# Earlier first loads, the norm as a row, and gate work laid between projection pieces in a hybrid encoder block

## The chip, the cores and the metric

The kernel runs on one NeuronCore of one Trainium2 chip. The metric is device time in microseconds (us) of one launch; lower is better. The times before are the median of three runs; one further execution was taken with the hardware profiler, and everything said of single instructions comes from it.

Five engines work side by side, each on its own queue in order: TensorE (PE in the profile, its weight loads PEld) multiplies and transposes, VectorE (DVE) and ScalarE (ACT) do elementwise work, GpSimd (POOL) fills and issues some transfers, SyncE (SP) issues most DMA transfers. PE writes to PSUM, eight banks of 128 x 512 fp32.

## The reference

All of it is fp32, with 256 tokens and a model width of 2048. The layer is a modulated block with two parallel sequence mixers:

```python
mod = silu(c) @ ada_w + ada_b                     # shift, scale, gate for two sub-layers
h = rms_norm(x, norm_mix_w) * (1 + scale_m) + shift_m
proj = h @ w_in                                   # one wide projection
...
h_a = bidirectional(mlstm_chunkwise, (q_a, k_a, v_a), ...)       # 4 heads, input and forget gates
qkv = silu(centred_depthwise_conv(b_qkv, gdn_conv_w))            # 5 taps along the tokens
beta = sigmoid(dir_heads(b_beta, B_HEADS))
log_decay = -exp(A_log) * softplus(dir_heads(b_a, B_HEADS) + dt_bias)
o_b = bidirectional(gated_delta_chunkwise, (q_b, k_b, v_b), ...)  # 16 heads
y_b = (rms_norm(o_b) * silu(b_z)) @ w_branch_b
...
x = x + gate_m * ((g_a * y_a + g_b * y_b) @ w_out)
x = x + gate_f * SwiGLU(rms_norm(x) * (1 + scale_f) + shift_f)
out = rms_norm(x, norm_final_w)
```

`proj` is split into q, k, v, output gate and gates of the mLSTM branch, q|k|v, z, beta and decay of the delta-rule branch ("heads" below), and merge gates.

## The kernel before

**Front (lines 73 to 98).** The vector c is loaded as one row `c1` of a 32-row zeroed tile, on ACT's DMA queue behind nothing in the program (the scheduler put it third, behind `cst` and `pk`). PE multiplies it by ones to spread it over 128 partitions; a Silu writes `row_c`. `c1` has a pool of its own, `w00`, which is closed at line 98, so that its space goes to the next pool, `w0`.

**First projection (lines 236 to 276).** Both halves of x, token by token in rows, are loaded as `xt` (1 MB each, SP queue). ACT squares them with a running sum (into parts of `x` as a throw-away), takes the root; DVE inverts it and scales `xt` by it; PE transposes `xt` in 32 pieces, ACT copies the results to `x` (channels on partitions, 16 blocks of 128 channels x 256 tokens). Then, for each block b of 16: two rows of `ada2` (`ra`, 1 MB each) and 16 column blocks of `w_in` (`raw`, 1 MB) are loaded; DVE forms the block's scale and shift as products with `row_c` (line 270), ACT applies both at once (line 271), `split` writes the block as a high part `hh` (ACT) and a rest `hl` (DVE), and PE accumulates 16 outputs `first[o]` in all eight banks with plain fp32 matmuls (line 274). `ra` has five slots (the two `xt` use the first two), `raw` has three.

**Gates (lines 279 to 344).** `first[0]` holds the gate pre-activations, `first[1..12]` q, k, v of heads 0 to 3, `first[13..15]` a part of the mLSTM's q and k. `gdn_conv` (line 217) evicts one output twice (to a padded tile and, scaled by the centre tap, to `cv`), adds four taps on DVE, and applies a Silu. Six convolutions come first in the program, then the gates: a polynomial for softplus, exponentials, `alpha_d` to DRAM (from where `gdn_phase1` reads it back), two scans, and the transpose `ptr` that yields `bT`, `eT` and `mT`.

**The rest of the projection in pieces.** `fjob` and `tjob` (lines 122 and 143) are generators. A `tjob` takes four 1 MB loads `raw`, and for each half load makes a high part `wh` (ACT, line 153) and a rest `wl` (DVE, line 154), three slots each, then issues 12 matmuls (lines 159 to 161): one piece. z of the delta-rule branch, v, the output and merge gates are such jobs. `fills` is the list of jobs with no deadline, and `fill(n)` takes n pieces. After the gates the program runs the eight pieces of z's first job, takes two fill pieces, and then (lines 637 to 644) works through heads 0 to 3 (`gdn_phase1`) and the first block inversion with fill pieces between their steps.

**What sets the order.** The Tile framework places instructions on each engine's queue by program order as a priority, but lets one that its own timing model sees ready go ahead of one that is not; waits are put in by it. A tile of a rotating pool waits until the last user of its slot is done. A DMA that waits for a slot holds up all later ones of its queue.

Of the kernel before, what the change touches and what calls it, by code (L numbers as in the profile page):

```python
# [9 lines left out]
F32 = mybir.dt.float32  # L10
# [40 lines left out]
def hybrid_block(ctx: ExitStack, tc: tile.TileContext, xr, nfr, crow, pk_d, cst_d, ada2, ada4, win0, winb, wint, wba, wbb, wo, wgu, wd, out, dbg=None):  # L51
# [16 lines left out]

    def gps(name):
        return g_ps.tile([P, 512], F32, tag="g", name=name)  # L70
# [23 lines left out]
    for g in range(4):  # L94
        pc_ = acc_ps.tile([P, 512], F32, tag="acc", name=f"crow{g}")
        PE.matmul(pc_, ones[0:32], c1[:, g * 512 : (g + 1) * 512], start=True, stop=True)
        S.activation(row_c[:, g * 512 : (g + 1) * 512], pc_, AF.Silu)
    s0.close()
# [44 lines left out]
    def tjob(name, chunks, xh, xl, done):  # L143
# [3 lines left out]
        for u, src in enumerate(chunks):  # L147
            raw = st.tile([P, 4, 512], F32, tag="raw", bufs=3, name=f"raw_{name}_{u}")
            nc.sync.dma_start(raw, src)
            for k0 in range(0, 4, 2):  # L150
                wh = st.tile([P, 2, 512], F32R, tag="wh", bufs=3, name=f"wh_{name}_{u}_{k0}")
                wl = st.tile([P, 2, 512], F32R, tag="wl", bufs=3, name=f"wl_{name}_{u}_{k0}")
                S.activation(wh, raw[:, k0 : k0 + 2], AF.Copy)  # L153
                V.tensor_tensor(wl, raw[:, k0 : k0 + 2], wh.bitcast(F32), ALU.subtract)  # L154
                for k in range(2):
                    kk = 4 * u + k0 + k
                    for t in range(2):
                        c = slice(t * P, (t + 1) * P)
                        PE.matmul(ps[t], xh[:, kk, c], wh[:, k], start=kk == 0, stop=False)  # L159
                        PE.matmul(ps[t], xl[:, kk, c], wh[:, k], start=False, stop=False)  # L160
                        PE.matmul(ps[t], xh[:, kk, c], wl[:, k], start=False, stop=kk == last)  # L161
                if k0:
                    pump()
                    if u == len(chunks) - 1:
                        done(ps)
                yield True
# [43 lines left out]
    NP_ = 3  # L210
# [6 lines left out]
    def gdn_conv(h, j, ps):  # L217
# [13 lines left out]
        S.activation(cv, ps, AF.Copy, scale=w[2])  # L231
# [3 lines left out]

    with ExitStack() as s0:
        w0 = pool(s0, "w0")

        x = w0.tile([P, KB, T], F32, name="x")
        ss = w0.tile([P, 2], F32, name="ssx")  # L240
        xt = []
        for t in range(2):
            xt.append(w0.tile([P, D + 2], F32, tag="ra", bufs=5, name=f"xt{t}"))
            nc.sync.dma_start(xt[t][:, :D], xr[:, t])
        for t in range(2):
            junk = x[:, 8 * t : 8 * t + 8].rearrange("p b t -> p (b t)")
            S.activation(junk, xt[t][:, :D], AF.Square, accum_out=ss[:, t : t + 1])
        S.activation(ss, ss, AF.Sqrt, bias=epsc, scale=1.0 / D)
        V.reciprocal(ss, ss)
        for t in range(2):  # L250
            V.tensor_scalar(xt[t][:, :D], xt[t][:, :D], ss[:, t : t + 1], None, ALU.mult)
        for b2 in range(KB // 2):
            px = gps(f"pxx{b2}")
            for e in range(2):
                for t in range(2):
                    PE.transpose(px[:, e * T + t * P : e * T + (t + 1) * P], xt[t][:, (2 * b2 + e) * P : (2 * b2 + e + 1) * P], ident)
            S.activation(x[:, 2 * b2 : 2 * b2 + 2], px.rearrange("p (e t) -> p e t", e=2), AF.Copy)
        banks = [acc_ps.tile([P, 512], F32, tag="acc", name=f"first{i}") for i in range(4)]
        banks += [gps(f"first{i}") for i in range(4, 8)]
        first = [banks[o // 2][:, (o % 2) * T : (o % 2 + 1) * T] for o in range(N0)]  # L260
        for b in range(KB):
            ra = [w0.tile([P, D + 2], F32, tag="ra", bufs=5, name=f"ra{b}_{i}") for i in range(2)]
            for i in range(2):
                nc.sync.dma_start(ra[i], ada2[b, :, i])
            raw = st.tile([P, N0, P], F32, tag="raw", bufs=3, name=f"raw0_{b}")
            nc.sync.dma_start(raw, win0[b])
            m2 = w0.tile([P, 2], F32, tag="m2", bufs=3, name=f"m2_{b}")
            for i in range(2):
                f = 1.0 if i else pk[:, PK_NMIX + b : PK_NMIX + b + 1]
                V.scalar_tensor_tensor(ra[i], ra[i], f, row_c, ALU.mult, ALU.mult, accum_out=m2[:, i : i + 1])  # L270
# [761 lines left out]
```

## Time and profile before

| | |
|---|---|
| median of three runs | 2219.57 us (2217.16 to 2230.97) |
| the profiled execution | 2226.21 us, span of its instructions 2224.4 us |
| PE busy | 2096.3 us, 94% of the span |
| DVE, ACT, POOL busy | 1408.9, 994.9, 103.6 us |
| read from HBM | 467.21 MB, 218 GB/s over the span |
| mean granted TensorE clock | 0.979 |
| PE's wait for `c1`, then for the transposes | 10.4 us, 14.0 us |
| PE's wait for the first split of z | 7.4 us |

The profile gives, for each group of instructions, its line, engine and operation, the tiles out<-in, shapes, count, busy us and mean ns, and after a second bar the idle time of the engine before them with what ended it. The timeline gives start and duration in us from the first instruction. In the stretches, the busy time of each engine is given with a count, then the granted clock (1.00 is full), the share of the DMA engines' time, and GB/s.

### The profile page before, as it was taken

What the parts mean: (1) busy time and instruction counts of PE and PEld (TensorE: products, weight loads), DVE (VectorE), ACT (ScalarE), POOL (GpSimd) and SP (SyncE); (2) the same over time, 40 slices, a digit from 0 to 9 for tenths busy, and PEclk for the clock granted to TensorE, in tenths of its full rate; (3) what the DMA queues carried; (4) which work ended last, traced back from release to release, by engine and by line L of the source; (5) the groups of instructions that cost most, each with busy time, mean ns of one, the idle gap of its engine ahead of it and who ended that gap; (6) DMA issues with size and microseconds to landing.
All of it is one profiled execution on the core that took longest, in us unless ns stands there. A gap on an engine that the chain in (4) does not pass through costs nothing.

```text
span 2224.4 us, 27756 instructions
## 1 busy us (share of the span) xinstructions
PE 2096.3 (94%) x10756; PEld 1754.7 (79%) x10756; DVE 1408.9 (63%) x2120; ACT 994.9 (45%) x1399; POOL 103.6 (5%) x206
## 2 busy tenths in 40 slices
PE   5989989998998899989999999989999999999997
PEld 4867778978887888778787787868888888878886
DVE  4677777886788677845557776564544454454454
ACT  3146436644564456434443444444444444444443
POOL 0002101100210111010000000000000000000000
PEclk9999999999999999999999999999999999999999
DMA  8976665675667455756787676545555555555553
GB/s 308 416 303 194 184 215 187 204 248 191 192 236 241 163 189 205 255 201 231 286 318 269 241 291 232 186 141 191 190 183 191 191 190 183 192 199 189 192 197 122
DMA packets 82645, 485.83 MB, mean 218 GB/s; under 512 B 10681, under 2 KB 21057, under 8 KB 28113
## 3 DMA queue, kind: packets, MB, share of 16 engines
q1 hardware_dynamic: 68672, 459.34, 58.0%
q0 software_dynamic: 6496, 9.49, 2.7%
q10 hardware_dynamic: 7346, 15.24, 1.8%
q8 instruction: 84, 1.38, 0.2%
q14 instruction: 47, 0.39, 0.0%
HBM read 467.21 MB, written 16.82 MB: 218 GB/s over the span
## 4 chain that ended last, share of the span: by engine, by line
PE 60%; DVE 4%; DMA 3%; issue 2%; ACT 1%; POOL 0%; DVEq 0%; ACTq 0%; POOLq 0%
PE acc_gt L159 4%; PE acc_gt L160 4%; PE acc_up L161 4%; PE acc_up L160 4%; PE acc_up L159 4%; PE acc_d L160 4%; PE acc_gt L161 4%; PE acc_d L159 4%; PE acc_d L161 4%; PE acc_o L160 2%; PE acc_o L161 2%; PE acc_o L159 2%; DMA ada<-ada 1%; PE acc_ya L160 1%; PE acc_ya L159 1%
## 5 line engine op out<-in xcount | busy, mean ns | idle before, releaser
L154 DVE TENSOR_TENSOR wl_up<-raw_up,wh_up 128x1024 fp32r<-128x1024 f32 x88 | 107.9, 1226 | 128.7 <-ACT wh_up L153 128.7
L154 DVE TENSOR_TENSOR wl_d<-raw_d,wh_d 128x1024 fp32r<-128x1024 f32 x88 | 107.8, 1226 | 123.2 <-ACT wh_d L153 123.2
L154 DVE TENSOR_TENSOR wl_gt<-raw_gt,wh_gt 128x1024 fp32r<-128x1024 f32 x88 | 107.8, 1225 | 109.3 <-ACT wh_gt L153 109.3
L107 DVE SCALAR_TENSOR_TENSOR ada<-ada,crow 128x2048 f32<-128x2048 f32 x64 | 146.2, 2284 | 39.2 <-DMA ada<-ada 39.2
L135 PE MATMUL acc_b<-hh,wh_b 128*128 128x256 f32 x576 | 167.3, 290 | 0.0
L137 PE MATMUL acc_b<-hh,wl_b 128*128 128x256 f32 x576 | 162.5, 282 | 1.1 <-DVE wl_b L132 1.1
L136 PE MATMUL acc_b<-hl,wh_b 128*128 128x256 f32 x576 | 162.9, 283 | 0.0
L153 ACT ACTIVATE wh_d<-raw_d 128x1024 fp32r<-128x1024 f32 x88 | 93.3, 1061 | 138.9 <-PE acc_d L160 132.0
L153 ACT ACTIVATE wh_gt<-raw_gt 128x1024 fp32r<-128x1024 f32 x88 | 93.3, 1060 | 133.9 <-PE acc_gt L160 78.9
L153 ACT ACTIVATE wh_up<-raw_up 128x1024 fp32r<-128x1024 f32 x88 | 93.2, 1060 | 117.8 <-PE acc_up L160 84.6
L159 PE MATMUL acc_gt<-wh_gt,hfh 128*128 128x512 f32 x352 | 138.8, 397 | 1.3 <-ACT hfh L183 1.1
L160 PE MATMUL acc_gt<-wh_gt,hfl 128*128 128x512 f32 x352 | 139.4, 396 | 0.0
L161 PE MATMUL acc_gt<-wl_gt,hfh 128*128 128x512 f32 x352 | 138.7, 394 | 0.0
L159 PE MATMUL acc_d<-wh_d,ffh 128*128 128x512 f32 x352 | 137.4, 390 | 0.0
L160 PE MATMUL acc_d<-wh_d,ffl 128*128 128x512 f32 x352 | 137.4, 390 | 0.0
L161 PE MATMUL acc_d<-wl_d,ffh 128*128 128x512 f32 x352 | 137.0, 389 | 0.0
L161 PE MATMUL acc_up<-wl_up,hfh 128*128 128x512 f32 x352 | 136.9, 389 | 0.0
L159 PE MATMUL acc_up<-wh_up,hfh 128*128 128x512 f32 x352 | 136.9, 389 | 0.0
L160 PE MATMUL acc_up<-wh_up,hfl 128*128 128x512 f32 x352 | 136.9, 389 | 0.0
L274 PE MATMUL first<-x,raw 128*128 128x256 f32 x512 | 111.6, 380 | 2.0 <-ACT x L271 2.0
L135 PEld LDWEIGHTS acc_b<-hh,wh_b 128*128 128x128 f32 x576 | 110.6, 192 | 2.1 <-issue 1.4
L137 PEld LDWEIGHTS acc_b<-hh,wl_b 128*128 128x128 f32 x576 | 110.8, 192 | 1.7 <-DVE wl_b L132 1.7
(339 smaller groups left out, 5375.8 us busy)
## 6 DMA issues: line engine op xcount, KB each, us to landing
ada<-ada SPq DMA_DIRECT2D x64, 1024.0 KB, 5.4
raw_gt<-wgu SPq DMA_DIRECT2D x44, 1024.0 KB, 4.9
raw_up<-wgu SPq DMA_DIRECT2D x44, 1024.0 KB, 4.9
raw_d<-wd SPq DMA_DIRECT2D x44, 1024.0 KB, 4.8
raw_b<-winb SPq DMA_DIRECT2D x36, 1024.0 KB, 5.4
ra<-ada SPq DMA_DIRECT2D x32, 1025.0 KB, 12.7
raw<-win SPq DMA_DIRECT2D x16, 1024.0 KB, 10.5
raw_z<-wint SPq DMA_DIRECT2D x16, 1024.0 KB, 5.8
```

Source lines behind the costliest of these rows:

```text
L107: V.scalar_tensor_tensor(raw, raw, 1.0, row_c[:, :D], ALU.mult, ALU.mult, accum_out=mod[:, c0 + b : c0 + b + 1])
L135: PE.matmul(o, wh[:, k], hh[:, kk], start=kk == 0, stop=False)
L136: PE.matmul(o, wh[:, k], hl[:, kk], start=False, stop=False)
L137: PE.matmul(o, wl[:, k], hh[:, kk], start=False, stop=kk == KB - 1)
L153: S.activation(wh, raw[:, k0 : k0 + 2], AF.Copy)
L154: V.tensor_tensor(wl, raw[:, k0 : k0 + 2], wh.bitcast(F32), ALU.subtract)
L159: PE.matmul(ps[t], xh[:, kk, c], wh[:, k], start=kk == 0, stop=False)
L160: PE.matmul(ps[t], xl[:, kk, c], wh[:, k], start=False, stop=False)
L161: PE.matmul(ps[t], xh[:, kk, c], wl[:, k], start=False, stop=kk == last)
L274: PE.matmul(first[o], raw[:, o], x[:, b], start=b == 0 and o % 2 == 0, stop=b == KB - 1 and o % 2 == 1)
```

## The change

`c1` becomes one row in a slot of `raw`, first on ACT's queue and without zeroed rows; the matmul contracts over one row. SP's order is pinned: both `xt`, then for each block `raw` before its two `ra`. `xt` is transposed as loaded, and DVE, not ACT, evicts the transposes; the inverse root becomes a row over the tokens, spread over the partitions by a matmul with a diagonal (`dg`, `rows`), and enters each block in one new DVE operation together with the scale; ACT then adds only the shift. The rest `hl` of a block is taken one block later. The squares go to a third slot of `ra` (`junk`).

`tjob` gets `early`: so many first splits are made, pinned in order, before its banks are taken; z's first job makes three. z and the fill jobs are in `fills` before the gates start. The gates become a generator with twelve steps, one piece after each, the six convolutions standing between the gate operations. `evict` copies the outputs to four pads (three before) ahead of the convolutions, which read the centre tap from the pad. Where before eight pieces of z and two more ran before the heads, now eight and four do. The job definitions move up unchanged.

`order(ins)` pins an instruction behind the one that precedes it in the program on its engine; it adds no wait.

```diff
-    s0 = ExitStack()
-    w00 = pool(s0, "w00")
-    c1 = w00.tile([32, D], F32, name="c1")
-    V.memset(c1, 0.0)
-    S.dma_start(c1[0:1], crow.unsqueeze(0))
+    c1 = st.tile([1, D], F32, tag="raw", bufs=3, name="c1")
+    S.dma_start(c1, crow.unsqueeze(0))
...
-        PE.matmul(pc_, ones[0:32], c1[:, g * 512 : (g + 1) * 512], start=True, stop=True)
+        PE.matmul(pc_, ones[0:1], c1[:, g * 512 : (g + 1) * 512], start=True, stop=True)
...
+        def halves(u, k0):
...
+            order(S.activation(wh, raws[u][:, k0 : k0 + 2], AF.Copy), early)
+            order(V.tensor_tensor(wl, raws[u][:, k0 : k0 + 2], wh.bitcast(F32), ALU.subtract), early)
+            return wh, wl
+
+        todo = [(u, k0) for u in range(len(chunks)) for k0 in (0, 2)]
+        made = [halves(*q) for q in todo[:early]]
+        if early:
+            yield True
...
-    NP_ = 3
+    NP_ = 4
...
+        if ps is not None:
+            S.activation(pd[:, 2 : T + 2], ps, AF.Copy)
         cv = fr.tile([P, T], F32, tag="cv", bufs=2, name=f"cv{h}_{j}")
-        S.activation(pd[:, 2 : T + 2], ps, AF.Copy)
-        S.activation(cv, ps, AF.Copy, scale=w[2])
+        S.activation(cv, pd[:, 2 : T + 2], AF.Copy, scale=w[2])
...
+        if ps is None:
+            evict(3 * h + j + 1 + NP_)
...
+    def gates(w0, zz, first):
+        evict(1)
+        order(V.tensor_scalar(zz, first[0], pk[:, PK_GB : PK_GB + 1], sgn, ALU.add, ALU.mult))
+        for o in range(2, NP_ + 1):
+            evict(o)
...
+        S.activation(tr[0:32, 0], zz[0:32], AF.Sigmoid)
+        yield
+        gdn_conv(0, 0, None)
+        yield
...
+            order(nc.sync.dma_start(xt[t][:, :D], xr[:, t]))
+        junk = w0.tile([P, D + 2], F32, tag="ra", bufs=5, name="junk")
+        for t in range(2):
+            order(S.activation(junk[:, :D], xt[t][:, :D], AF.Square, accum_out=ss[:, t : t + 1]))
...
+            V.tensor_copy(x[:, 2 * b2 : 2 * b2 + 2], px.rearrange("p (e t) -> p e t", e=2))
+        V.reciprocal(ss, ss)
+        dg = w0.tile([P, T], F32, name="dgx")
+        for t in range(2):
+            V.tensor_scalar(dg[:, t * P : (t + 1) * P], ident, ss[:, t : t + 1], None, ALU.mult)
+        prow = acc_ps.tile([P, 512], F32, tag="acc", name="prow")
+        PE.matmul(prow[:, :T], ones, dg, start=True, stop=True)
+        order(S.activation(rows, prow[:, :T], AF.Copy))
...
+            order(nc.sync.dma_start(raw, win0[b]))
+            for i in range(2):
+                order(nc.sync.dma_start(ra[i], ada2[b, :, i]))
+            m2 = w0.tile([P, 2], F32, tag="m2", bufs=3, name=f"m2_{b}")
+            f = pk[:, PK_NMIX + b : PK_NMIX + b + 1]
+            order(V.scalar_tensor_tensor(ra[0], ra[0], f, row_c, ALU.mult, ALU.mult, accum_out=m2[:, 0:1]))
+            order(V.scalar_tensor_tensor(x[:, b], x[:, b], m2[:, 0:1], rows, ALU.mult, ALU.mult))
+            order(V.scalar_tensor_tensor(ra[1], ra[1], 1.0, row_c, ALU.mult, ALU.mult, accum_out=m2[:, 1:2]))
+            order(S.activation(x[:, b], x[:, b], AF.Identity, bias=m2[:, 1:2]))
+            order(S.activation(hh[:, b], x[:, b], AF.Copy))
+            for bb in ((b - 1,) if b < KB - 1 else (b - 1, b)):
+                if bb >= 0:
+                    order(V.tensor_tensor(hl[:, bb], x[:, bb], hh[:, bb].bitcast(F32), ALU.subtract))
...
+        zj = z_job(0, 3)
+        next(zj)
+        fills[:] = [zj] + rest
+        zz = w0.tile([P, T], F32, name="zz")
+        for _ in gates(w0, zz, first):
+            fill(1)
...
-    run(z_job(0))
-    fills[:] = rest
-    fill(2)
```

More of the change, by code (lines that the diff above doesn't have):

```diff
@@ L67, in big, with order @@
         return p.tile([P, KB, T], dt, tag="b16", name=name)
+    def order(ins, yes=True):
+        return tc.keep_in_program_order(ins) if yes else ins
     def gps(name):
@@ L598, in steps @@
                 yield
-    rest = [a_vo(0, h) for h in range(NH_A)]
-    for i in range(4):
-        rest += [m_job(1, i), a_vo(1, i)] + [a_qk(i, j) for j in range(4) if i or j == 3] + [m_job(0, i)]
     def drive(gen, n=2):
```

233 lines of the change are left out of this document (115 added, 118 removed).

## The prediction

> **What bounds the kernel now.** I read the page's first part, then busy time by stretch, then the timeline of the two stretches that the edit touches.
>
> ```profile
> span 2224.4 us, 27756 instructions
> PE 2096.3 (94%) x10756; PEld 1754.7 (79%) x10756; DVE 1408.9 (63%) x2120; ACT 994.9 (45%) x1399; POOL 103.6 (5%) x206
> ```
> TensorE (PE) is the bound: 94% of the span. The edit neither adds nor removes matmuls worth counting, so it can win only PE's idle time and its time at half clock. Columns below: stretch and its us; busy us (count) of PE, weight loads, VectorE (DVE), ScalarE (ACT), POOL; granted clock; DMA share; GB/s.
>
> ```profile
> 0.00:39.40 39.40, 13.68 (x40) 8.39 (x40) 14.08 (x16) 15.80 (x23) 1.11 (x9) 1.00 0.75 282
> 39.40:151.70 112.30, 111.55 (x512) 96.95 (x512) 76.07 (x83) 21.47 (x42) 0.00 (x0) 1.00 0.96 393
> 151.70:159.10 7.40, 0.03 (x1) 0.00 (x0) 6.72 (x14) 7.36 (x16) 0.00 (x0) 0.84 0.48 159
> 159.10:166.90 7.80, 6.27 (x14) 4.49 (x15) 7.43 (x15) 5.33 (x10) 0.00 (x0) 0.50 0.33 101
> 166.90:200.90 34.00, 33.12 (x157) 27.07 (x156) 26.93 (x57) 21.70 (x31) 6.44 (x13) 1.00 0.69 193
> 200.90:254.00 53.10, 51.12 (x204) 38.93 (x203) 39.72 (x96) 30.34 (x49) 9.11 (x18) 0.94 0.57 174
> 254.00:317.60 63.60, 56.91 (x267) 45.87 (x266) 52.85 (x100) 24.11 (x25) 8.42 (x16) 1.00 0.79 264
> ```
> Four stages are to be seen: a front of 39.4 us with 13.7 us of PE; the first projection, where PE looks full but DMA is too (0.96); a hole of 7.4 us; then 7.8 us at clock 0.50. After 167 us PE is nearly full, and what comes earlier there shifts the end one for one, unless another engine falls behind.
>
> **The front, and why the loop ends when it does.**
>
> ```profile
> 0.74 1.34 SPq L266 DMA_DIRECT2D raw<-win  x3
> 10.43 7.16 PE L96 MATMUL crow<-c,ones 32*128 32x512 f32 x8 [10.43 <-DMA c<-crow]
> 17.63 0.80 SPq L244 DMA_DIRECT2D xt<-xr  x2
> 22.56 1.91 ACT L247 ACTIVATE x<-xt 128x2048 f32<-128x2048 f32 x1 [2.82 <-DMA xt<-xr]
> 24.38 0.19 ACT L247 ACTIVATION_READ_ACCUMULATOR x<-xt 128x1 f32 x1
> 27.06 1.28 ACT L248 ACT_TABLE_LOAD   x1
> 31.58 6.58 PE L256 MATMUL pxx<-cst,xt 128*128 128x128 f32 x32 [13.99 <-issue]
> 38.75 0.61 ACT L271 ACTIVATE x<-x,m 128x256 f32<-128x256 f32 x1
> 46.62 0.33 SPq L266 DMA_DIRECT2D raw<-win  x1
> 131.61 2.35 DVE L270 SCALAR_TENSOR_TENSOR ra<-ra,pk,crow 128x2050 f32<-128x2050 f32 x1 [1.14 <-DMA ra<-ada]
> 139.06 2.35 DVE L270 SCALAR_TENSOR_TENSOR ra<-ra,pk,crow 128x2050 f32<-128x2050 f32 x1 [1.12 <-DMA ra<-ada]
> 143.90 0.60 ACT L271 ACTIVATE x<-x,m 128x256 f32<-128x256 f32 x1 [6.42 <-DVE ra L270]
> 144.56 7.17 PE L274 MATMUL first<-x,raw 128*128 128x256 f32 x32 [0.30 <-ACT x L271]
> L233 DVE SCALAR_TENSOR_TENSOR cv<-pad,pk,cv 128x256 f32<-128x256 f32 x32 | 13.9, 478 | 3.2 <-ACT cv L231 3.1
> ```
> SP issues three `raw` loads, then no load until 17.63, because `x`'s space is that of `c1`, which PE reads until 17.6; PE itself waited 10.4 us for `c1`, third on ACT's queue. In steady state a block's three 1 MB loads take 139.06 - 131.61 = 7.45 us, 2.48 each, and DVE waits for each: DMA paces the loop, PE needs about 6.9 of the 7.45.
>
> *Step 1, loads and row of c.* With `c1` first on ACT's queue I put its landing at 4 us: `xt`, issued into an empty queue at 17.63, was used at 22.56, 4.9 us later with 2.48 of transfer, so about 2.4 of latency after 0.7, and a little for the neighbours. The loss of the memset before `c1` and of 31 zero rows is worth nothing on PE (same 512 columns). Row of c: 4.0 + 7.2 = 11.2, last Silu 11.9. Both `xt` lie there by 10. The Squares are pinned behind the Silus: 2 x (1.91 + 0.19) = 4.2, to 16.1; table (1.28) and root, put at 1.6, to 17.7; reciprocal and two diagonal products on DVE, put at 0.6, to 18.3. Transposes run meanwhile (11.2 to 17.8 at the 6.58 us of before), now evicted by DVE in eight copies that follow them and end near 18, so at no cost; at 1.5 us each they would outlast their cover by 5.
>
> *Step 2, norm as a row.* One matmul and one copy (about 1.2 us) run under the first `ra` product (2.35, to 20.7). The new scaling is one DVE operation per block, 0.48 by the row of `cv` (same operation, same shape), hidden in the 7.45 us, where DVE has 76.07 / 16 = 4.8 us of work; at the loop's end it lies under the load of the second `ra`. Then the second product 2.3 and the Identity 0.6: the first block of x is ready at 24.1 instead of 39.4 (38.75 + 0.61). The two whole-token scalings that go were ahead of the transposes; that gain is in the sum already. The order of splits costs nothing: hl of the block before needs no wait.
>
> *Step 3, the DMA's next stop.* `raw` has three slots and `c1` now takes one early and frees it at 11.2. The load for block 3 waits for block 0's matmuls, as the issue at 46.62 does (39.4 + 6.9). Here that is 24.2 + 6.9 = 31.1. Queued before it are eleven loads and the constants, 3 + 11.5 x 2.48 = 31.5: they run out just then. From there: latency 2.4, 39 loads x 2.48 = 96.8, product 2.4, Identity 0.6, issue 0.3: last block at 134 against 144.5 (143.90 + 0.60), a gain of 10. The bound from the other side: PE rests from 17.8 to 24.2, and the stretch of 0.50 after the 7.4 us hole shows what such a rest may do. At half clock block 0 ends 3.4 later (7.8 us at half lose 3.9), DMA stops for as long, and the gain is 6.6.
>
> The Trainium skill, page "TensorE: Matmul & The Clock Gate", section "What's actually happening", says that PE falls to half clock after an idle window of about 3.4 us and returns after about 3.4 us of work. By that rule the rest costs 1.7 us (an estimate from this page), by the row 3.4 to 3.9. The trace agrees on the fall and shows 7.8 us to the return, not 3.4, so the row stands.
>
> I take 8.5 (6.6 to 10): loop ends on PE at 143.2 instead of 151.7.
>
> **The hole behind the loop.**
>
> ```profile
> 147.11 0.54 DVE L288 TENSOR_SCALAR zz<-first,pk,cst 128x256 f32<-128x256 f32 x1
> 148.10 1.28 ACT L333 ACT_TABLE_LOAD   x1
> 149.39 0.42 ACT L333 ACTIVATE tr<-zz 32x256 f32<-32x256 f32 x1
> 158.03 2.01 ACT L153 ACTIVATE wh_z<-raw_z 128x1024 fp32r<-128x1024 f32 x2
> 177.21 0.42 ACT L310 ACTIVATE alr<-sp 32x256 f32<-32x256 f32 x1
> 184.16 1.28 ACT L571 ACT_TABLE_LOAD   x1
> 188.69 0.18 DVE L344 COPY mT<-ptr 128x32 f32<-128x32 f32 x1
> PE acc_z L159 <- ACT wh_z L153: 7.4, 1, 7.4
> PE acc_z L161 <- DVE wl_z L154: 1.5, 1, 1.5
> DMA to landing us min/median/max: 4.9/6.5/9.6
> ```
> PE waits for z's first split, which ACT makes at 158 behind evictions, convolutions and table loads.
>
> *Step 4, three splits early.* They are pinned behind the last hh and hl. The second z load needs the slot of block 14, free at 143.2 - 7.2 = 136, and lands 4.9 later (the last row, of the issues at line 149 from 130 to 200 us: shortest, median and longest) at 141. Third split 1.0 on ACT (two took 2.01) and 1.22 on DVE (row below), then zz 0.54, which frees PE's bank: z starts at about 144.2, a hole of 1.0: gain 6.4. ACT and DVE stand behind that third split for about 2 us, with evictions and `zz` queued behind; the two earlier splits and hl fill part of it. With the hole gone, so are the 1.5 us wait and the half clock (3.9): gain 5.4. Steps 1 to 4: 8.5 + 6.4 + 5.4 = 20.3.
>
> *Step 5, what is given back.* The hole was where ACT and DVE did convolutions undisturbed.
>
> ```profile
> 146.70:188.90 42.20, 32.42 (x131) 25.69 (x130) 36.11 (x75) 31.98 (x50) 3.18 (x5) 0.88 0.50 155
> 188.90:254.00 65.10, 63.12 (x266) 48.87 (x266) 48.49 (x115) 37.69 (x62) 12.38 (x26) 0.95 0.62 183
> 159.10:200.90 41.80, 11.71 (x49) 9.24 (x50) 0.00 (x0) 0.91 0.62 176
> 200.23 0.39 PE L160 MATMUL acc_v<-wh_v,hl 128*128 128x512 f32 x1
> 200.46 0.39 PE L161 MATMUL acc_v<-wl_v,hh 128*128 128x512 f32 x1
> L154 DVE TENSOR_TENSOR wl_z<-raw_z,wh_z 128x1024 fp32r<-128x1024 f32 x8 | 9.8, 1221 | 1.6 <-ACT wh_z L153 1.6
> PE p L467 <- issue: 5.0, 1, 5.0
> ```
> The third row is of v's tile alone: by 200.9 PE had done z's 96 matmuls and 49 of v, that is 12 pieces of 12. A matmul follows the last one by 0.23 (200.23, 200.46), a piece of 12 by 2.75 (33 for 12), so PE alone could have 12 pieces at 144.2 + 33 = 177, 24 us early. DVE can't follow: gates, six convolutions and splits were 36.1 us of a stretch of 42.2. Starting behind hl of the last block, about 137, and losing some 2 us to the z load, DVE ends the same work (two more splits, 2.4, against six convolution steps of head 2, at 13.9 / 32 = 0.43, that now come later) at 175 packed full, at 181 packed as before: 8 to 14 us earlier than 188.7, not 24. PE then waits for wl, or later for the heads. Behind it DVE has room (48.5 of 65.1) and can recover part; the chain of the first inversion, where PE waits 5.0 us already, takes the rest. The cost is 0 (DVE recovers all) to 12 (DVE's shift decides); I take 6, the middle, as no row is nearer. Reordering of fills moves two pieces (5.5 us of PE work) ahead; they are missing later, where a flush of pieces has no need of them: nothing. A fourth pad, POOL's memsets and the moved definitions: POOL is 5% busy, nothing. The convolution's centre tap now reads the pad, so ACT's two operations follow one another: at most 0.4 x 6 on an ACT with 10 us free.
>
> The Trainium skill, "ScalarE: Activation LUTs", section "What ACT_TABLE_LOAD costs", gives 1.28 us for a load plus 1.38 us of drain. Six loads stand in this stage, from 148.10 to 184.16, and convolutions strewn between gates invite as many; by that rule ACT would need 32.0 + 6 x 1.4 = 40 of 42 us (an estimate from this page) and become the bound. The rows differ: the load at 148.10 takes 1.28, and the next operation starts at 149.39, without a drain.
>
> Sum: 20.3 - 6 = 14.3 us. The profiled execution took 2226.2 (span 2224.4 and 1.8 around it), which gives 2211.9; it lies 6.6 over the median of the three runs, 2219.6, against which I predict 2219.6 - 14.3 = 2205.
>
> **Rivals.**
> *Full gain.* DVE's room after 189 covers step 5, PE stays warm: 10 + 6.4 + 5.4 = 22: 2198. For: DVE 74% busy there. Against: the inversion's chain.
> *No gain in front.* If `c1` lands with the loads queued on SP, near 10 as before, the Silus, Squares and first block move by 6, and with them the fourth `raw` and the loop's end: 8.5 becomes 2.5, total 8: 2211. For: `c1` did come at 10.4. Against: two larger loads were ahead of it on its queue.
> *Slower.* The pieces come out strictly between gate steps: a convolution (0.4 for its scaled copy on ACT, 4 x 0.43 on DVE, 1.28 + 0.42 for a table and Silu) is followed by wh and wl (2.2), 6.0 us a piece where PE needs 2.75. Three early pieces, nine at 6.0: 152.4 + 54 = 206 against 200.9, 5.5 us late: 2225. It decides from 5.4 us a piece ((200.9 - 152.4)/9). For: few buffers (three wh) and many tables. Against: in before the gate operations run wherever an engine is free (the Sigmoid of `tr` at 149.4 ahead of all polynomials).
>
> **How the numbers follow.** Forecast (2199 to 2211) 0.47; full gain 0.25; no gain in front 0.15; slower 0.10; 0.03 for something worse. The range runs from the full gain, less the 2.4 us by which the lowest run lies under the median, to front and step 5 both at their worse ends (2.5 + 6.4 + 5.4 - 12 = 2.3): 2195 to 2217. More than 1% (22 us, about what a measurement of this kernel tells from no change) needs under 2197: half of the full gain and some of its tail, 0.18. Slower by 1% needs over 2242: 0.03. Within: 0.79.
>
> **What would show it.** Steps 1 and 2: PE's first loop matmul at 24 us, no DMA pause before 17 us. Step 3: last x block at 134 to 138, clock 0.5 near 24 or not. Step 4: hole under 1.5 us, no half clock behind it. Step 5: twelfth piece between 180 and 188, more waits of PE for wl, the gap before the first inversion product over 5 us. The prediction is wrong if the hole only moves behind z's third piece, or if the rows of 254 to 460 lose what the front won.

## The result and the profile after

The changed kernel takes 2201.31 us, the median of eight runs (2196.56 to 2221.85); on the same chip the kernel before takes 2222.97 (2217.16 to 2233.02, eight runs). The ratio is 0.9905, with a 95% interval of 0.9882 to 0.9929: some 21 us faster, against a forecast of 14.3.

One execution can't be read for so small a difference. The profiled execution of the changed kernel is the longest of the eight:

```profile
span 2220.1 us, 27749 instructions
PE 2114.5 (95%) x10758; PEld 1770.0 (80%) x10758; DVE 1416.0 (64%) x2141; ACT 995.1 (45%) x1395; POOL 104.9 (5%) x209
```

Its span is only 4.3 us under that of before (2224.4), though the median is 21 better. Its mean clock was 0.969, that of before's profile 0.979. So the same kernel ran once more with the experiments (first experiment below); this execution had a clock of 0.979, like before's, and is the one to lay beside it. Its first lines:

```profile
span 2198.3 us, 27749 instructions
PE 2102.0 (96%) x10758; PEld 1757.6 (80%) x10758; DVE 1416.3 (64%) x2141; ACT 994.8 (45%) x1395; POOL 105.1 (5%) x209
```

PE's work is about that of before (10,758 matmuls against 10,756); what went is time in which PE did nothing. By stretch of the same execution (columns as in the prediction: PE, weight loads, DVE, ACT, POOL, clock, DMA share, GB/s):

```profile
0.00:23.20 23.20, 13.57 (x43) 8.36 (x43) 11.57 (x20) 10.08 (x14) 2.42 (x12) 0.95 0.94 375
23.20:145.20 122.00, 116.54 (x513) 98.12 (x514) 85.41 (x97) 19.46 (x41) 0.00 (x0) 0.98 0.95 388
145.20:165.20 20.00, 18.74 (x76) 13.41 (x75) 18.34 (x39) 16.25 (x27) 0.64 (x1) 1.00 0.53 184
165.20:186.80 21.60, 19.03 (x84) 15.63 (x84) 18.84 (x40) 17.95 (x23) 5.86 (x12) 0.92 0.65 166
186.80:226.90 40.10, 40.10 (x183) 31.77 (x183) 34.62 (x82) 28.23 (x52) 6.07 (x12) 1.00 0.59 176
226.90:303.40 76.50, 67.69 (x296) 53.31 (x295) 60.22 (x124) 28.70 (x33) 11.52 (x22) 0.98 0.71 243
```

The front is 23.2 us long instead of 39.4, and the first projection takes 122.0 us instead of 112.3: of the 16.2 us won in front, 6.5 are left when the loop ends. The hole of 7.4 us is gone, and the half clock behind it is one stretch of 3.4 us (in the row with clock 0.92) instead of 7.8. PE is full from 186.8 to 226.9. What it waited for up to 320 us (engine and line, by whom, us in all, times, longest):

```profile
PE first L435 <- ACT x L429: 10.3, 13, 4.9
PE p L568 <- issue: 7.3, 1, 7.3
PE acc_z L173 <- DVE wl_z L156: 3.1, 2, 2.6
```

The wait ahead of the first inversion product, 5.0 us before, is 7.3. The profile names no releaser for it ("issue"), but the timeline shows the chain: the inversion, made on DVE in a tile `uu`, is stored to `inv_d`, read back as `ut`, and transposed on DVE before PE starts at 303.4.

```profile
290.22 0.56 POOL L547 DMA_DIRECT2D inv_d<-uu  x1 [39.22 <-DVE uu L544]
295.96 4.36 POOL L557 DMA_DIRECT2D ut<-inv_d  x8 [5.18 <-DMA inv_d<-uu]
302.51 0.71 DVE L560 STREAM_TRANSPOSE ut<-ut 128x512 f32<-128x512 f32 x1 [5.04 <-DMA ut<-inv_d]
```

PE has no more pieces 6.2 us after `uu` is done, in both kernels. From the store's issue to the issue of the first read it is 5.7 us, in before 3.3 (306.73 to 310.07), and that is the growth of the wait.

### The profile page after: what moved, and what is told of

Read it like the earlier page. It is cut to its first block, busy times and chain, and to the rows that moved or that the text cites. A ratio compares the mean times of both kernels' runs of the same rounds, so it can differ in the third digit from the quotient of the medians.

```text
span 2220.1 us, 27749 instructions
## 1 busy us (share of the span) xinstructions
PE 2114.5 (95%) x10758; PEld 1770.0 (80%) x10758; DVE 1416.0 (64%) x2141; ACT 995.1 (45%) x1395; POOL 104.9 (5%) x209
## 4 chain that ended last, share of the span: by engine, by line
PE 63%; DVE 5%; DMA 4%; issue 2%; ACT 1%; POOL 1%; DVEq 0%; SPq 0%; ACTq 0%; POOLq 0%
PE acc_gt L171 4%; PE acc_gt L172 4%; PE acc_up L172 4%; PE acc_up L173 4%; PE acc_up L171 4%; PE acc_d L172 4%; PE acc_d L173 4%; PE acc_gt L173 4%; PE acc_d L171 4%; PE acc_o L172 2%; PE acc_o L173 2%; PE acc_o L171 2%; PE acc_ya L172 1%; PE acc_ya L171 1%; PE acc_ya L173 1%
## 5 line engine op out<-in xcount | busy, mean ns | idle before, releaser
L435 PE MATMUL first<-x,raw 128*128 128x256 f32 x512 | 118.0, 392 | 10.5 <-ACT x L429 10.5
L435 PEld LDWEIGHTS first<-x,raw 128*128 128x128 f32 x512 | 99.5, 196 | 29.0 <-ACT x L429 14.9
L131 ACT ACTIVATE wh_b<-raw_b 128x1024 fp32r<-128x1024 f32 x72 | 76.1, 1060 | 88.9 <-PE acc_b L136 52.7
## 6 DMA issues: line engine op xcount, KB each, us to landing
ra<-ada SPq DMA_DIRECT2D x32, 1025.0 KB, 10.7
```

Of the source, the lines that this page charges most:

```text
L131: S.activation(wh, raw[:, k0 : k0 + 8], AF.Copy)
L435: PE.matmul(first[o], raw[:, o], x[:, b], start=b == 0 and o % 2 == 0, stop=b == KB - 1 and o % 2 == 1)
```

## The experiments

Runs of one kernel differ by 15 us and more, and most of that is the clock: over the 75 runs of the kernel before (2213.1 to 2244.5 us, clock 0.968 to 0.981) the correlation of time and granted clock is -0.89. So two results are given: the ratio of the medians with its interval, on the chip of that run, and a difference at equal clock, from one line through the 197 runs of all kernels with a level for each kernel and one slope (-1.99 us for 0.001 of clock; spread around it 2.7 us, intervals of 95%). The second takes out a clock that a variant itself causes, too. A level for each of the three chips of these runs moves the results by under 1 us. At equal clock the change is worth -20.6 ± 1.5 us. That is the measure for its parts. The ratios are against the kernel before, and so are the differences at equal clock of the front alone and the gates alone; all later differences are against the changed kernel.

From each one's profile come the leads over before: how much sooner than in before a place of the program was reached, in us. The places are the loop's last matmul, z's first, the end of the twelfth piece, the first matmul of the first inversion, the end of the last piece of the merge gates, and the end of the span.

| | loop end | z starts | 12th piece | inversion | gates' last piece | span |
|---|---|---|---|---|---|---|
| before, at us | 151.7 | 159.1 | 200.9 | 317.6 | 1157.3 | 2224.4 |
| changed, its first profile | 4.3 | 12.0 | 12.3 | 10.5 | 3.0 | 4.3 |
| changed, again | 6.5 | 14.3 | 14.1 | 14.2 | 22.1 | 26.1 |
| front alone | -0.6 | 7.1 | 4.1 | 4.2 | 4.4 | 4.6 |
| gates alone | -0.2 | 7.5 | 3.8 | 2.9 | 10.4 | 11.0 |
| no early splits | 4.0 | 11.8 | 10.0 | 9.4 | 17.7 | 21.5 |
| ten pieces | 5.6 | 13.4 | 12.3 | 15.6 | 24.2 | 27.6 |
| fill(9) | 6.8 | 14.6 | 14.7 | 14.2 | 6.9 | 9.3 |
| warm | 3.7 | 11.4 | 11.4 | 12.0 | 10.9 | 13.3 |
| no taps | 5.5 | 13.2 | 15.7 | 14.3 | 15.8 | 20.0 |
| warm, own bank | 7.0 | 14.8 | 14.8 | 14.9 | 19.5 | 22.8 |
| no row | 7.6 | 15.4 | 15.6 | 15.6 | 19.6 | 22.6 |
| gates unbroken | 7.7 | 15.4 | 2.3 | 1.8 | 6.3 | 10.5 |
| late loads | -3.9 | 3.9 | 4.3 | 4.5 | 3.6 | 6.6 |

In the first three columns two profiles of one kernel differ by some 2 us, in the fourth by up to 4; the last two carry the clock of that execution as well.

**The changed kernel again.** No edit.

> The changed kernel once more, for a second profile. Theory: the profiled execution of it was long (2221.9, clock 0.969, 138 us of half clock against 97 in the profile of before), and a half-clock us costs half a us of PE; an execution at clock 0.978 to 0.980 takes 2197 to 2203, about 20 less than before, and its lead at the first inversion product is 10 to 14 us, hardly less at the end. Rival: the lead of 10.5 us at the first inversion is lost by the later stages themselves (two fill pieces fewer), so that the lead at z's last job is near zero again whatever the clock, and the median gain comes from elsewhere.

Measured: 2211.92 us against 2224.3, ratio 0.9926 (0.9896 to 0.9956). The two measurements of the same kernel agree within their intervals, and the profile is the one shown above. The leads of the first profile fall from 10.5 at the inversion to 3.0 at the gates' last piece, those of the second rise from 14.2 to 22.1; the first had 137.5 us at half clock, the second 93.5, before 96.6.

**The front alone.** Jobs, gates and pads as before; loads, row of c, norm and scaling as changed.

```diff
-    def tjob(name, chunks, xh, xl, done, early=0):
+    def tjob(name, chunks, xh, xl, done):
...
-    NP_ = 4
+    NP_ = 3
...
```

> Only the early loads, the order of loads and the norm as a row; gates, convolutions and z as before. Theory: PE ends the first loop 4 to 10 us earlier (143.2 was forecast for 151.7, 147.4 was profiled), the hole of 7.4 us and the half clock behind it stay, and the kernel is 4 to 9 us faster than before: 2214 to 2218 if before is at 2222. Rival: the front is paced by what follows (DVE's gates and the inversion's chain start no earlier), gain under 2.

Measured: ratio 0.9968 (0.9945 to 0.9991), -10.8 ± 1.6 us at equal clock. The way was not the one expected: the loop ended at 152.3, not sooner than before. The gain stands at z's start, which lies at 152.0 instead of 159.1. The code of z's splits is that of before here. The timeline of this kernel, start and duration, shows where they went:

```profile
145.13 7.17 PE L282 MATMUL first<-x,raw 128*128 128x256 f32 x32 [1.80 <-ACT x L276]
145.43 1.04 ACT L152 ACTIVATE wh_z<-raw_z 128x1024 fp32r<-128x1024 f32 x1
146.50 1.23 DVE L153 TENSOR_TENSOR wl_z<-raw_z,wh_z 128x1024 fp32r<-128x1024 f32 x1 [0.52 <-ACT wh_z L152]
151.95 0.58 PE L158 MATMUL acc_z<-wh_z,hh 128*128 128x512 f32 x1
```

ACT makes z's first split at 145.4, under the loop's last block; in before it stood at 158.0 behind the gates. The hole of before was a place in ACT's order, and with the changed front the framework chose another one by itself.

The same happened in front, to this run's cost. The gates' Exp `ea`, which the changed kernel pins inside the gates, was put ahead of the Silus of the row of c here:

```profile
12.58 0.20 ACT L298 ACTIVATE ea<-pk 128x1 f32<-128x1 f32 x1 [9.14 <-DMA pk<-pk]
12.81 1.28 ACT L98 ACT_TABLE_LOAD   x1
14.10 2.06 ACT L98 ACTIVATE crow<-crow 128x512 f32<-128x512 f32 x4
```

It waits for `pk`, and the four Silus end at 16.2, in the changed kernel at 10.6. The first block comes at 28.1 instead of 23.2, so this run shows less in front than the changed kernel has there.

**The gates alone.** Jobs and gates as changed; the front as before.

```diff
-    c1 = st.tile([1, D], F32, tag="raw", bufs=3, name="c1")
+    c1 = w00.tile([32, D], F32, name="c1")
...
-            order(V.scalar_tensor_tensor(x[:, b], x[:, b], m2[:, 0:1], rows, ALU.mult, ALU.mult))
...
```

> Front as before; early splits, gates and convolutions between pieces as changed. Theory: loop ends on PE at 151.7 as before, hole under 1.5 us, and the kernel is 8 to 14 us faster than before (6.4 + 5.4 less what DVE and the inversion's chain take). Rival: nothing of the hole reaches the end, since the inversion's chain hangs on the gates' end and not on PE: gain under 3.

Measured: ratio 0.9981 (0.9958 to 1.0005), -9.1 ± 1.7 at equal clock. The sum of the parts, 10.8 + 9.1 = 19.9, is near 20.6, but not place by place: each alone closes the hole (7.1 and 7.5 at z's start), and together they have that once, and 6.5 at the loop's end that neither has alone. The front alone lacks that in part because of its late `ea`.

**No early splits.**

```diff
-        zj = z_job(0, 3)
-        next(zj)
+        zj = z_job(0)
```

> As changed, but z's first job makes no splits early. Theory: the pinned early splits close the hole: without them the first z matmul comes 2 to 5 us after the loop's last (program order still puts z's first piece behind the first gate step only), PE falls to half clock or not, and the kernel is 2 to 6 us slower than the changed one. Rival: with z in the list of pieces from the start the scheduler makes the splits as early anyway: within 1 us of the changed one.

Measured: ratio 0.9934 (0.9907 to 0.9962); +1.7 ± 2.1 against the changed kernel at equal clock. z starts at 147.3 and the loop ends at 147.7, so there is no hole here either. By the code `early` pins the order of all eight splits of z's first job, not of three alone, and this run leaves out both. Together they are worth 0 to 4 us, not the hole.

**Ten pieces.** The last two steps of the gates take no piece, so that ten instead of twelve stand ahead of the heads, as before.

```diff
-        for _ in gates(w0, zz, first):
-            fill(1)
+        for n, _ in enumerate(gates(w0, zz, first)):
+            if n < 10:
+                fill(1)
```

> As changed, but the last two gate steps take no piece, so that ten pieces stand before the heads, as before. What is asked: how much of the gain is gates and pieces overlapped, and how much that all later fill pieces stand two places further on. Theory (formed on the profiles of the single parts): with twelve pieces the waits of PE at 677 us (6.7 for a split of z's third job) and half of the one at 950 (10.5 down to 6) go, so with ten they come back: 5 to 10 us slower than the changed kernel, while its lead at the first inversion product stays within 3 us of the changed one's. Rival (the prediction): the two pieces are worth nothing, within 2 us.

Measured: 2205.11 us, ratio 0.9897 (0.986 to 0.9934); +3.6 ± 2.4 against the changed kernel at equal clock. The two measures disagree: the ratio is a little better than that of the changed kernel, the adjusted level worse. The wait ahead of the first inversion falls from 7.3 to 5.1 and the inversion starts 1.4 sooner (302.0), which is near what separates any two profiles. What the two pieces are worth stays between 0 and 6. Of the two later waits that were expected back, one came: PE waits for a split of z's third job again. From 640 to 700 us, first before, then the changed kernel, then this one:

```profile
PE acc_z L161 <- DVE wl_z L154: 7.4, 2, 6.7
PE acc_z L173 <- DVE wl_z L156: 0.6, 1, 0.6
PE acc_z L173 <- DVE wl_z L156: 8.0, 2, 6.3
```

The wait ahead of the fourth inversion did not come back: it is 6.8 here, 10.7 in before and 6.1 in the changed kernel.

**Nine pieces ahead of each inversion** instead of six, to fill PE's wait there.

```diff
-        fill(6)
+        fill(9)
```

> As changed, but nine fill pieces in place of six ahead of each of the four first inversion products, where PE waits 7.3, 5.3, 5.3 and 6.1 us. Theory: at the first inversion the chain over DVE and DMA is late, not PE: the three pieces (8.2 us of PE) fill the waits, the lead of PE that step 5 lost there is kept, and the kernel is 10 to 24 us faster than the changed one (the waits, and the 7 us at half clock behind each). Rival: the splits of the added pieces hold up the chain on DVE by as much (3 x 1.2 us) and the gaps move behind: within 4 us.

Measured: 2214.92 us, ratio 0.9931 (0.9904 to 0.9958); +6.8 ± 2.2 against the changed kernel at equal clock. The first wait shrinks, 7.3 to 1.4, but the inversion starts at 303.4 as before: the chain over DVE and DMA sets it, not PE. The later waits grow: between 460 and 1130 us PE waited in the two kernels, first this one, then the changed one,

```profile
PE p L568 <- DVE ut L560: 22.2, 4, 9.8
PE acc_z L173 <- DVE wl_z L156: 14.5, 4, 6.7
```

```profile
PE p L568 <- DVE ut L560: 16.7, 3, 6.1
PE acc_z L173 <- DVE wl_z L156: 1.2, 2, 0.6
```

A reading that fits is that the pieces bring their splits to DVE when the next group's chain needs DVE; no run separates it from the other places that all later pieces take. That PE is idle ahead of an inversion does not make the time free.

**PE kept warm in front.** Eleven idle matmuls into the other half of the bank of `prow`, to cover PE's rest ahead of the first block.

```diff
         PE.matmul(prow[:, :T], ones, dg, start=True, stop=True)
+        for _ in range(11):
+            PE.matmul(prow[:, T:], ones, cst[:, 0:T], start=True, stop=True)
         order(S.activation(rows, prow[:, :T], AF.Copy))
```

> As changed, with eleven matmuls of constants (0.43 us each at full clock) on PE between the norm's row and the first block, where PE rests 4.85 us. Theory: the rest drops the clock for 7 to 10 us, delays block 0's matmuls, with them the fourth load of win0, and with it the loop; kept warm, the loop on PE ends 2 to 4 us earlier (141.5 to 143.5 in place of 145.2 to 147.4) and the kernel is 2 to 4 us faster. Rival: the loop's end is set by DMA alone or PE is not kept warm by this: end of the loop within 1 us of 145.

Measured: 2209.95 us, ratio 0.993 (0.9898 to 0.9961); +6.1 ± 2.1 at equal clock. The copy of `rows` out of the same bank waited for all eleven, and the first block started at 26.3 instead of 23.2. That wait is one of the program: the copy waits for a semaphore that the row's own matmul doesn't raise here, only the last of the eleven does (at 22.59; in the next run the row's matmul does, at 18.36). So this run tells nothing about the clock, and the next one gives the eleven a bank of their own:

```diff
         order(S.activation(rows, prow[:, :T], AF.Copy))
+        pwarm = acc_ps.tile([P, 512], F32, tag="acc", name="pwarm")
+        for _ in range(11):
+            PE.matmul(pwarm[:, :T], ones, cst[:, 0:T], start=True, stop=True)
```

> The kept-warm front again, with the eleven matmuls of constants in a PSUM bank of their own, so that the copy of the norm's row no longer waits for them (in the last run it did, and the first block came 3 us later). Theory: no half clock from 19 to 30 us, block 0's matmuls end at about 30.5 instead of 33.5, the fourth load of win0 is issued 2 to 3 us earlier, and PE ends the loop at 141.5 to 144 instead of 145 to 147; kernel 2 to 4 us faster than the changed one. Rival: loop end within 1 us of 145: the load stream decides, or later waits do.

Measured: 2205.49 us, ratio 0.9904 (0.9869 to 0.994); +1.0 ± 2.6 at equal clock. PE now stays warm. The first stretch and the loop, and the load for block 3:

```profile
0.00:23.20 23.20, 18.22 (x64) 12.45 (x64) 11.54 (x20) 10.05 (x14) 2.41 (x12) 1.00 0.93 371
23.20:144.70 121.50, 114.27 (x513) 96.49 (x514) 85.56 (x97) 19.47 (x41) 0.00 (x0) 1.00 0.97 390
```

```profile
30.41 0.33 SPq L424 DMA_DIRECT2D raw<-win  x1
```

The clock is 1.00 from the first to the last matmul of the loop, and block 3's load is issued at 30.41 instead of 32.69. Yet the loop ends at 144.7 instead of 145.2 (147.4 in the first profile of the changed kernel). So the half clock in front costs the loop's end 0.5 to 2.7 us, about what two profiles differ by, and not 3.4.

**Gates without the side taps.** The six convolutions of heads 0 and 1 leave out their four side taps: 24 DVE operations, 0.43 us each by the row in the prediction.

```diff
-        for i in (0, 1, 3, 4):
+        for i in (0, 1, 3, 4) if h > 1 else ():
```

> As changed, but the convolutions of heads 0 and 1 leave out their four side taps (24 operations, 10.4 us of DVE, in the gate stage; the output is then another). Theory (step 5): DVE sets the gates' end, and with it the heads and the first inversion: alpha is stored and the first inversion begins 4 to 9 us earlier than in the changed kernel, which is 3 to 8 us faster. Rival: PE or the table loads on ACT set the pace: under 2 us at the first inversion product and at the end.

Measured: 2206.43 us, ratio 0.9896 (0.9854 to 0.9938); +2.4 ± 2.6 against the changed kernel at equal clock. Its stretches from the loop's end to the twelfth piece, to 226.1, and to the inversion:

```profile
146.20:185.20 39.00, 34.87 (x151) 27.06 (x150) 31.04 (x56) 29.47 (x48) 6.49 (x13) 1.00 0.66 197
185.20:226.10 40.90, 40.90 (x193) 32.90 (x192) 32.00 (x81) 27.54 (x49) 6.08 (x12) 1.00 0.58 167
226.10:303.30 77.20, 67.68 (x296) 53.32 (x295) 60.12 (x123) 28.80 (x33) 11.54 (x22) 0.98 0.70 238
```

DVE has 31.0 us of work up to the twelfth piece, against 18.34 + 18.84 = 37.2 in the changed kernel. The twelfth piece ends 39.0 us after the loop instead of 41.6, 1.7 of which is the half clock that is missing here (clock 1.00 against 0.92 over 21.6 us). The inversion starts at 303.3 as with the taps (303.4). PE's idle time up to the twelfth piece is still 4.1 us (39.0 - 34.9), with the taps 3.8.

**The norm without its row.** Tokens scaled ahead of the transposes as before, the scale back in the Identity; loads and order as changed.

```diff
-            V.tensor_copy(x[:, 2 * b2 : 2 * b2 + 2], px.rearrange("p (e t) -> p e t", e=2))
...
-            order(V.scalar_tensor_tensor(x[:, b], x[:, b], m2[:, 0:1], rows, ALU.mult, ALU.mult))
...
-            order(S.activation(x[:, b], x[:, b], AF.Identity, bias=m2[:, 1:2]))
+            order(S.activation(x[:, b], x[:, b], AF.Identity, scale=m2[:, 0:1], bias=m2[:, 1:2]))
```

> As changed, with the norm as before (tokens scaled ahead of the transposes, ACT evicts, ACT applies scale and shift); early loads and gates stay. Theory: the root and the scalings (two of 1.3 us) stand ahead of the transposes again, the transposes end 8 us later, at 24 to 25 instead of 16.5, and hold the slots of both xt until then: DMA pauses, the first block comes at 28 to 31 and the loop on PE ends 5 to 8 us later than in the changed kernel; kernel 4 to 8 us slower than it. Rival: the row is worth nothing, since DMA runs out at block 3 in either case: within 2 us.

Measured: 2207.63 us, ratio 0.9921 (0.9889 to 0.9953); +4.0 ± 2.4 at equal clock. The first block starts at 24.6 instead of 23.2, the loop ends at 144.1 instead of 145.2, and all leads up to the inversion are as large as with the row. No place up to there shows a gain by the row; where 4 us should come from later, no profile shows.

**Gates unbroken.** The same gates, all ahead of the twelve pieces in the program.

```diff
         for _ in gates(w0, zz, first):
-            fill(1)
+            pass
+        fill(12)
```

> As changed, with the three early splits, but gates and convolutions in one go ahead of the twelve pieces in program order. Theory: the place of the pieces in the program closes the hole, more than the early splits (leaving these out cost 2 us): PE does its three made pieces without a hole (8.2 us), then waits 4 to 8 us for the fourth, which ACT makes behind the gates; kernel 3 to 8 us slower than the changed one, but faster than before. Rival: the scheduler mixes them by readiness anyway: within 2 us.

Measured: 2218.06 us, ratio 0.9962 (0.9937 to 0.9988); +6.5 ± 2.1 at equal clock, at a clock that is itself lower (mean 0.973 against 0.976). Its stretches around 152 us:

```profile
144.00:152.30 8.30, 8.28 (x37) 6.44 (x35) 6.77 (x14) 7.93 (x15) 0.00 (x0) 1.00 0.51 180
152.30:167.90 15.60, 0.02 (x1) 0.05 (x1) 15.42 (x42) 12.28 (x20) 3.17 (x5) 0.63 0.24 53
167.90:198.60 30.70, 30.70 (x126) 25.48 (x126) 18.32 (x30) 17.41 (x25) 3.32 (x8) 0.85 0.55 181
```

PE runs through the three splits that were made early, then does nothing for 15.6 us while DVE works 15.4 on gates. The lead of 15.4 at z's start is 2.3 at the twelfth piece. The place of the pieces between the gate steps is what keeps the hole away.

**Late loads.** `c1` again with its memset, 32 rows and a space of its own that is given to the projection afterwards.

```diff
-    c1 = st.tile([1, D], F32, tag="raw", bufs=3, name="c1")
+    s0 = ExitStack()
+    w00 = pool(s0, "w00")
+    c1 = w00.tile([32, D], F32, name="c1")
+    V.memset(c1, 0.0)
+    S.dma_start(c1[0:1], crow.unsqueeze(0))
...
+    s0.close()
```

> As changed, but c1 as before: 32 zeroed rows in a pool of their own, whose space is that of the first projection's tiles. Theory: xt waits for the row of c on PE again; but pinned in order, raw now stands behind xt on SP's queue, so that nothing is loaded before 17 us, not even the three raw of before: first block at 38 to 42, loop end on PE at 155 to 160, kernel 8 to 15 us slower than the changed one, 5 to 12 faster than before at most. Rival: c1 lands as early as in the changed kernel (first on the queue of ACT but for the scheduler's choice), the front shifts by under 4 us.

Measured: 2218.09 us, ratio 0.9959 (0.9939 to 0.9979); +9.2 ± 2.0 at equal clock. From its timeline:

```profile
4.74 7.16 PE L100 MATMUL crow<-c,ones 32*128 32x512 f32 x8 [4.74 <-DMA c<-crow]
11.93 0.86 SPq L401 DMA_DIRECT2D xt<-xr  x2
17.03 1.09 PE L410 MATMUL pxx<-cst,xt 128*128 128x128 f32 x4 [5.13 <-DMA xt<-xr]
```

The row of c is only 1.8 us later (4.74 against 2.93). What costs is the space: SP's first load is issued at 11.93, when the last matmul on `c1` ends, the first block starts at 32.0, and the loop ends at 155.6 instead of 145.2, 10.4 later. The early loads are the front's gain.

## Why the prediction was right, and which of its steps failed

*Steps 1 and 2* came out as worked: the first block of x at 23.76 in the changed kernel's first profile (23.2 in the second) for 24.1. Rows of the first, start and duration:

```profile
2.93 7.16 PE L97 MATMUL crow<-c,ones 1*128 1x512 f32 x8 [2.93 <-DMA c<-crow]
10.02 6.60 PE L406 MATMUL pxx<-cst,xt 128*128 128x128 f32 x32
20.47 0.48 DVE L427 SCALAR_TENSOR_TENSOR x<-x,m,rows 128x256 f32<-128x256 f32 x1
23.76 21.49 PE L435 MATMUL first<-x,raw 128*128 128x256 f32 x85 [4.85 <-ACT x L429]
33.84 0.33 SPq L421 DMA_DIRECT2D raw<-win  x1
```

`c1` came at 2.93, sooner than the 4.0 put, so the rival without a gain in front is gone. The row's operation took the 0.48 put for it.

*The size.* The gain is 20.6 at equal clock and 21.7 between the medians, against 14.3 put. That the time (2201) lies so near the 2205 is in part luck: the forecast was taken off 2219.6, a median of three runs, and the median of eight is 2223.0; from that the forecast would be 2208.7 and the full gain 2201.

*Step 3* is the term that was mis-sized: 8.5 put, 4.3 and 6.5 in the two profiles. The rest of PE (4.85 us) and the half clock behind it came as the worse bound said, and block 3's load was issued at 33.84 (32.69 in the second profile) for 31.1. But the bound priced it too high: with PE warm the loop ends 0.5 to 2.7 sooner, not 3.4. What failed is "39 loads x 2.48" from there on without a break. From the issue of block 3's load to the last block of x the sum has 2.4 + 96.8 + 2.4 + 0.6 + 0.3 = 102.5 us; it took 106.4 and 105.3 in the two profiles and 107.1 with PE warm. SP's queue waited for slots, the load of `raw` for PE's last use of it, in before, in the changed kernel's second profile and with PE warm:

```profile
SPq L266 <- PE first L274: 61.8, 13, 7.0
```

```profile
SPq L421 <- PE first L435: 85.8, 13, 12.5
```

```profile
SPq L424 <- PE first L438: 84.3, 13, 10.2
```

and the loop's loads moved at 388 GB/s against 393 in before's loop. Before and after by stretches inside the loop, first before:

```profile
39.40:60.00 20.60, 20.59 (x95) 18.16 (x96) 14.15 (x17) 3.46 (x7) 0.00 (x0) 1.00 0.95 367
60.00:100.00 40.00, 40.00 (x187) 35.20 (x186) 27.16 (x27) 5.93 (x12) 0.00 (x0) 1.00 1.01 422
100.00:140.00 40.00, 39.55 (x183) 34.18 (x182) 26.82 (x27) 5.25 (x11) 0.00 (x0) 1.00 1.01 420
```

```profile
23.20:60.00 36.80, 35.09 (x150) 29.90 (x151) 23.82 (x28) 4.07 (x9) 0.00 (x0) 0.94 0.94 376
60.00:100.00 40.00, 38.40 (x172) 31.88 (x170) 29.54 (x34) 5.03 (x11) 0.00 (x0) 1.00 1.01 417
100.00:137.00 37.00, 35.16 (x158) 29.70 (x159) 26.23 (x28) 4.21 (x10) 0.00 (x0) 1.00 0.98 404
```

Before's stream is slow for its first 20.6 us alone; the changed one moves 376 GB/s for 36.8 us and 404 at the end, where before has 420. With PE warm the same three stretches have 406, 409 and 384 and nearly the same end, so the loss moves rather than goes. A reading that fits: `raw` now stands ahead of its two `ra` on SP's queue, waits for a slot of three blocks earlier, and holds both back. No run separates this from the rest. That the loads, and not the first block alone, set the loop's end is seen in pairs: without the row the first block is 1.4 later (24.6) and the end 1.1 sooner (144.1); with the front alone the first block is at 28.1, 11.3 sooner than in before, and the end 0.6 later, with the slowest stream of all:

```profile
28.10:152.30 124.20, 116.28 (x513) 98.12 (x514) 86.47 (x102) 20.87 (x43) 0.00 (x0) 0.98 0.90 364
```

*Step 4*, the hole: 6.4 put, 14.3 - 6.5 = 7.8 found at z's start. The size held; the reason given, three pinned splits, did not: the pinning is worth 0 to 4 us. Without them, and with the front alone, the hole is closed too. The prediction took the order on ACT for given wherever nothing pinned it. Of the 5.4 for what comes behind the hole, the half clock fell from 7.8 us to one stretch of 3.4 us, while a wait for z's `wl` stayed (3.1 us in all, 1.5 before).

The Trainium skill, page "TensorE: Matmul & The Clock Gate", section "What's actually happening", was set against a row here: full clock after about 3.4 us of work. In the first profile the clock was half from 19.4 to 29.6 with work from 23.76, so 5.8 us of work; in the second from 21.0 to 27.9 with work from 23.2, so 4.7. Both lie between the page's figure and the 7.8 of before's row. The work lost, half of it, is 2.9 and 2.4 us, where the prediction had 1.7 by the page and 3.4 to 3.9 by the row.

*Step 5*, 6 us given back, with DVE as the reason, failed. Up to the twelfth piece the lead stays what it was at z's start (14.3 and 14.1), and the inversion has 14.2; so the 5.4 and the -6 about cancel, as the prediction had it, and the lead at the inversion is, by chance of those terms, its 14.3. But taking 24 operations off DVE moved the inversion by nothing. PE itself fills the stage: 18.74 + 19.03 = 37.8 of 41.6 us, with 160 matmuls where the 12 pieces count 144. The prediction's bound, PE alone with 33 us, left out the other 16, the half clock and the waits for `wl`. ACT, which the prediction asked about for its table loads, made nine of them here instead of six and was busy 34.2 of the 41.6 us. The last row on v (295.6 before, 276.0 in the second profile) leads by 19.6, 5.4 more than the inversion: these are the two pieces (5.5 us) that stand ahead of the heads now, not a gain of PE's.

The rest of the gain comes after the inversion, where the prediction put nothing: 14.2 becomes 22.1 by the gates' last piece. Between these two places PE does the same work, and its idle time there fell from 59.3 to 47.1 us (839.7 - 780.4 and 831.8 - 784.7); 62.4 us of half clock against 54.1 took some of it back. Two waits make most of it. That for z's third job (6.7 us) is there in before, in the front alone, with ten pieces and with fill(9), and in no other kernel here. So the two pieces ahead of the heads take it away, which the prediction put at nothing. The wait ahead of the fourth inversion, from 900 to 980 us, first in before, then in the changed kernel,

```profile
PE p L467 <- DVE ut L459: 10.7, 1, 10.7
PE p L568 <- DVE ut L560: 6.1, 1, 6.1
```

is 10.0 with the front alone and 5.9 to 8.0 in every kernel with the changed gates. Which of their steps shortens it is open.

*The rivals.* Full gain (22 us, 2198) is nearer to the gain than the forecast, and as near to the time, but its mechanism, DVE's room, isn't what made it. "Slower" needed six microseconds a piece between gates; 12 pieces took 41.6, 3.5 each. The wait ahead of the first inversion did grow past 5, as asked for in the last part, but by the slower store, not by DVE. A hole behind z's third piece, the sign of being wrong, came only in the run with the gates unbroken.

## What to carry to other kernels

A wait of the bounding engine for an operation that another engine could have done earlier is a matter of that engine's order: see first whether the order moves by itself when something ahead of it moves, before pinning or adding anything. When a load stream paces a loop, look at when the stream starts and at what stops its queue: an earlier first matmul shortens the loop only as far as the loads come earlier, too. An idle stretch on the bounding engine ahead of a serial chain isn't free room when the filler needs the engine on which the chain runs.

## What the runs showed of the hardware

The spread of the times of the kernel before, 2213 to 2245 us over 75 runs on three chips, goes mostly with the granted clock: -2.0 us for 0.001. The half clock comes in stretches of about 3.4 us and multiples (3.4, 6.8, 10.2, 13.7, 17.1, 20.5 in the first profile of the changed kernel and in that of the unbroken gates), most of them just after a rest of PE of some microseconds. A single profile of the faster kernel showed a fifth of its gain. A tile that went from DVE through DRAM and a transpose to PE took 13.2 us from the store's issue (290.22) to PE's first product (303.4), in before 10.9 (306.73 to 317.6).
